# Half-at-a-time state-space tables on GpSimd, and attention scores in two 64-row halves, in a two-layer trunk on one core

## The chip, the core and the metric

One core of one Trainium2 chip. The metric is the device time of one execution in microseconds (us). The engines are named as in the profile: PE is TensorE (PEld its weight loads), DVE is VectorE, ACT is ScalarE, POOL is GpSimd, SP the engine whose queue issues the DMAs. b and h below are numbers of a state-space block and of an attention head.

## The reference

Two layers over a sequence of 256 rows and 2048 columns, all in float32:

```python
proj = x @ w_in[l]                    # 2048 x 4096: q, k, v, u of 1024 columns each
attn = diff_attention(q, k, v, lam)   # 8 heads, each two score maps of 64 columns
ssm  = s5_mixer(u, ...)               # 64 groups of 16 channels, 64 complex states, then a GLU
mix  = concat(group_rms_norm(attn), group_rms_norm(ssm)) @ w_out[l]
x = layer_norm(ALPHA * x + mix)
x = layer_norm(ALPHA * x + square(relu(x @ w_up[l])) @ w_down[l])
```

A head's output is (softmax(q0 k0) - lam softmax(q1 k1)) v, where q0, q1 and k0, k1 are the two 64-column halves of the head, and a row may only see keys of its own 64-row chunk and of earlier ones. The state-space part is a linear recurrence with a complex diagonal factor; the kernel turns it, with tables of cosines and sines of the state's angle, into real scans.

## The kernel before

**Products.** Each float32 product is made of three passes: a weight tile `w` is loaded by DMA (512 KB, 256 rows), ACT rounds it to `wh`, DVE makes the rest `wl = w - wh`, and PE multiplies hi by hi, hi by lo and lo by hi into one accumulator `acc` (`mms`, L209 to 215). There are four `wh` and four `wl` buffers (`WB`), so ACT's rounding waits until PE has used an older one, and PE waits for DVE and ACT. An `acc` instruction has 512 columns.

**A layer.** `mixer` (L836) makes the projections, attention, the state-space part, the GLU and most of `w_out`; `last_chunk` ends it with the layer norm; the MLP follows, 16 chunks of 512 columns, with `acc` matmuls back to back. In the mixer PE's order is written by a small planner (`Flow`): each task yields a test (a time, a free slot, an event), the planner's clock `fl.now` moves on with the instructions put out, and the first ready task of the highest priority goes next. Its constants (`L_PREP`, `L_SCAN`, `L_EXP`, ...) are how long other engines are thought to take. PE runs in exactly this order; the queues of DVE, ACT and POOL are ordered by the compiler's scheduler, and each engine runs its queue in order.

**State space.** 64 groups go in 8 blocks of 8 groups (b = 0 to 7, four pairs of groups each). `ssm_prep` (L455) makes a block's tables on POOL: `abc` (12 instructions of 128x64: the bases times the factor), two memsets, and `tab` (128 x 2 x 4 x 128 numbers) by doubling: step m = 0 to 6 makes n = 1, 2, ... 64 new columns from the n before, six instructions each. ACT spreads `abc` and the bases into `zx` and `cx`; PE transposes `zx` (`zT`) and makes a small kernel `pk`. `ssm_in` (L516) multiplies (PE, `X`, 64 rows at a time), then DVE multiplies X by the tables (16 instructions), scans (8, L542) and multiplies back; `ssm_out` (L552) makes `Y` on PE, DVE adds and the GELU goes through ACT and DVE. Blocks follow each other in one task: X of b+1 comes after Y of b. `tab` has two buffers, `abc` one.

**Attention.** `attn_block` (L583) handles one head and one block of 128 rows: scores `S` into PSUM, one matmul per half with all 128 rows of `kT` against a `qT` whose other half is zero (two `qT` tiles per four heads, written by `to_T`, L818, with `half8`), and one matmul of a one-row mask (`mq`, `mk`) added to it (L598). DVE takes the maximum (`mx`), ACT the exponentials (`pe`), DVE combines the halves; later PE transposes (`pT`) and multiplies by v. Two `S` tiles are in use.

**End of the mixer.** After Y of block 7: GELU, 16 transposes and splits (`uT`, `s`, `gS`), two GLU products, the group norm, and products by `w_out`; whatever of attention and `w_out` is still open fills PE meanwhile.

Of the kernel before, what the change touches and what calls it, by code (L numbers as in the profile page):

```python
# [9 lines left out]
F32 = mybir.dt.float32  # L10
# [8 lines left out]
P = 128  # L19
T = 256  # L20
# [16 lines left out]
UN = 19  # L37
# [13 lines left out]
L_PREP = 7.5  # L51
# [9 lines left out]
class Flow:  # L61
# [53 lines left out]
def trunk(ctx: ExitStack, tc: tile.TileContext, x, w_in, lambda_q1, lambda_k1, lambda_q2, lambda_k2,  # L115
# [13 lines left out]
    ps_a = pool("ps_a", 2, space=PSUM)  # L129
# [35 lines left out]
    half8 = const.tile([P, 2], F32, name="half8")  # L165
    G.memset(half8, 0.0)
    G.memset(half8[0:64, 0:1], HD ** -0.5)
    G.memset(half8[64:128, 1:2], HD ** -0.5)

    mq0 = rawp.tile([1, P], F32, tag="pe", name="mq0", bufs=4)  # L170
    G.memset(mq0, 0.0)
    G.memset(mq0[:, 0:CHUNK], 1.0)
    mk0 = rawp.tile([1, T], F32, tag="pe", name="mk0", bufs=4)
    G.memset(mk0, 0.0)
    G.memset(mk0[:, T - CHUNK:T], -1e30)
    mq = const.tile([1, P], F32R, name="mq")
# [175 lines left out]
    def lay_params(fl, p, l, loaded):  # L352
# [97 lines left out]
        p["nlam"] = nlam  # L450
        ts(p["vec"][:, 0:8], p["vec"][:, 0:8], 1.0 - lam_init, ALU.mult)

    def ssm_prep(fl, p, b):

        qs = slice(4 * b, 4 * b + 4)  # L455

        abc = ssm.tile([P, 4, 4, GC], F32, tag="abc", name="abc")
        tm = [ssm.tile([P, 4, NK // 2], F32, tag="tm", name="tm", bufs=2) for _ in range(2)]
        a_r, a_i = (p["ab"][:, i, qs].unsqueeze(2).to_broadcast([P, 4, GC]) for i in range(2))
        for o, base, s_re, s_im in ((0, p["base"][0], ALU.subtract, ALU.add), (2, p["base"][1], ALU.add, ALU.subtract)):  # L460
            z_r, z_i = base[:, 0, qs], base[:, 1, qs]
# [12 lines left out]
        for g in range(2):  # L474
            act(zx[:, :, :, 0, g], abc[:, 0:2], scale=half[:, g:g + 1])
            act(zx[:, :, :, 1, g], p["base"][0][:, :, qs], scale=half[:, g:g + 1])
            act(cx[:, 0:2, :, g], abc[:, 2:4], scale=half[:, g:g + 1])
            act(cx[:, 2:4, :, g], p["base"][1][:, :, qs], scale=half[:, g:g + 1])
        G.memset(tab[:, 0, :, 0:1], 1.0)
        G.memset(tab[:, 1, :, 0:1], 0.0)  # L480
        for m in range(7):
            n = 1 << m
            er, ei = (p["pw"][:, i, m + 1, qs].unsqueeze(2).to_broadcast([P, 4, n]) for i in range(2))
            u, v = tab[:, 0, :, 0:n], tab[:, 1, :, 0:n]
            t0, t1 = tm[0][:, :, 0:n], tm[1][:, :, 0:n]
# [28 lines left out]
        return bT, k0, cx, tab  # L514

    def ssm_in(fl, p, q, b, u):  # L516

        bT, k0, cx, tab = q
# [33 lines left out]
    def ssm_out(fl, p, q, b, u, h):  # L552

        bT, k0, cx, tab = q
# [28 lines left out]
    def attn_block(fl, p, h, qb, kT, qT, v, i, o, has, need, hold):  # L583

        yield lambda: need[0]() and fl.slot("S")() and fl.slot("hd")() and (qb > 0 or fl.slot("o")())
        if qb == 0:
            hold.append(fl.take("o"))
        give, leave = fl.take("S"), fl.take("hd")
        nk = P * (qb + 1)
        rr = sm.tile([P, 2], F32, tag="rr", name="rr", bufs=3)  # L590
        ri = sm.tile([P, 2], F32, tag="ri", name="ri", bufs=3)
        mx = sm.tile([P, 2], F32, tag="mx", name="mx", bufs=3)
        sp = ps_a.tile([P, 2, T], F32, tag="S", name="S")
        pe = [rawp.tile([P, T], F32, tag="pe", name="pe", bufs=4) for _ in range(2)]
        for s in range(2):
            TE.matmul(out=sp[:, s, 0:nk], lhsT=qT[s][:, h, qb * P:(qb + 1) * P], rhs=kT[:, h, 0:nk],  # L596
                      start=True, stop=False)
            TE.matmul(out=sp[:, s, 0:nk], lhsT=mq, rhs=mk[:, T - nk:T], start=False, stop=True)  # L598
        fl.now += 0.55 * (qb + 1)
        V.reduce_max(out=mx, in_=sp[:, :, 0:nk], axis=AX.X, negate=True)  # L600
        for s in range(2):
            act(pe[s][:, 0:nk], sp[:, s, 0:nk], AF.Exp, bias=mx[:, s:s + 1], accum_out=rr[:, s:s + 1])
        give(L_EXP)

        V.reciprocal(out=ri, in_=rr)
        stt(ri[:, 1:2], ri[:, 1:2], p["nlam"], rr[:, 0:1], ALU.mult, ALU.mult)
        stt(pe[0][:, 0:nk], pe[1][:, 0:nk], ri[:, 1:2], pe[0][:, 0:nk], ALU.mult, ALU.add)
# [3 lines left out]
        for k in range(qb + 1):  # L611
            TE.transpose(ps[:, k], pe[0][:, k * P:(k + 1) * P], ident)
# [205 lines left out]
    def to_T(fl, t, acc, dst, ev):  # L818
# [9 lines left out]
        if len(dst) == 1:  # L828
            act(dst[0][:, :, t * P:(t + 1) * P], ps)
        else:  # L830
            for s in range(2):
                act(dst[s][:, :, t * P:(t + 1) * P], ps, scale=half8[:, s:s + 1])
        give(L_EVAC)
        ev[t].set(L_EVAC)

    def mixer(l, p, xT, first):  # L836
        fl = Flow(tp=2, sx=2, S=2, hd=2, o=2)
# [31 lines left out]
        def attention(i):  # L869
            mA[i] = Split("mA", 1)  # L870
            for h in range(4):
                o = rawp.tile([P, NT, P], F32, tag="o", name="o", bufs=2)
                has, hold = events(NT), []
                for qb in range(NT):
                    need = both(*k_ev[i], *q_ev[i]), both(*v_ev[i])
                    fl.add(3, attn_block(fl, p, h, qb, kT[i], qT[i], v, i, o, has, need, hold))
                fl.add(2, attn_norm(fl, p, 4 * i + h, o, has, lambda hd, m=mA[i]: m(hd % 4), mA_ev[4 * i + h], hold))

        def steps(g, dt=0.65):
# [237 lines left out]
```

## Time and profile before

| | us |
|---|---|
| median of 3 runs | 2340.1 (2339.4 to 2340.41) |
| the profiled execution: its time, its span | 2340.92, 2339.1 |
| PE / DVE / ACT / POOL busy | 2234.1 / 1550.2 / 1080.6 / 446.6 |
| layer 0: first product of X with a table, to Y of block 7 read by DVE | 96.1 to 321.8 |
| from there to the first transpose of the MLP | 321.8 to 484.9 |
| layer 1: the same two stretches | 1246.2 to 1457.9, to 1636.1 |

Busy time is the sum of the instructions' durations without overlaps; a PE instruction's end is modelled, so on PE the distance from one start to the next says more. "Mean ns of one" includes what an instruction waits inside itself. A wait's releaser is who ended it last.

### The profile page before, as it was taken

The page shows a single profiled execution, that of the slowest core. Times are in us where ns is not written, and L with a number is a line of the kernel's source. Part 1 is how long each engine was busy: PE and PEld are TensorE (multiplying, and loading weights), DVE is VectorE, ACT ScalarE, POOL GpSimd, SP SyncE. Part 2 cuts the span into 40 slices and gives each one's busy share as a digit, 9 for nine tenths or more (in the row PEclk, how much of TensorE's full clock was granted, in tenths as well). Part 3 has the DMA queues.
Part 4 walks back from the last instruction along what each step waited for, and adds up shares of the span by engine and source line. Part 5 has one row for each costly group of instructions (what it writes and reads, how often), then busy time and mean ns, then how long its engine had stood idle before and what let it go on. Part 6 is the DMA issues. An engine that isn't in the chain of part 4 may idle for free.

```text
span 2339.1 us, 29790 instructions
## 1 busy us (share of the span) xinstructions
PE 2234.1 (96%) x10836; PEld 1803.0 (77%) x10836; DVE 1550.2 (66%) x2226; ACT 1080.6 (46%) x1521; POOL 446.6 (19%) x990
## 2 busy tenths in 40 slices
PE   8888899999999999999999888999999999999997
PEld 6666677778888878788877667777888888888886
DVE  4667878865555556556677888678555556555557
ACT  4444446354444444444444454654444444444443
POOL 1799900000000001610013983000000000000001
PEclk9998999999999999999999989999999999999998
DMA  8432334666766655565754324465666566666564
GB/s 255 126 97 85 100 123 149 206 183 189 197 199 188 205 179 185 162 195 183 240 157 146 115 73 127 135 195 156 189 189 190 188 196 184 186 194 189 187 198 144
DMA packets 227058, 396.57 MB, mean 170 GB/s; under 512 B 38336, under 2 KB 38496, under 8 KB 226912
## 3 DMA queue, kind: packets, MB, share of 16 engines
q1 hardware_dynamic: 226912, 394.68, 55.1%
q8 instruction: 85, 1.39, 0.2%
q14 instruction: 61, 0.50, 0.1%
HBM read 392.53 MB, written 2.10 MB: 169 GB/s over the span
## 4 chain that ended last, share of the span: by engine, by line
PE 73%; POOL 14%; DVE 6%; issue 3%; DMA 2%; ACT 1%; SPq 1%; DVEq 0%; ACTq 0%; POOLq 0%
PE acc L215 67%; POOL tm L134 9%; POOL tab L134 4%; PE tp L250 2%; PE acc L734 2%; DVE wl L134 1%; DMA w<-in_w_in 1%; DVE res L150 1%; DVE wk L134 1%; POOL abc L134 1%; ACT wh L153 1%; PE S L596 1%; DMA w<-in_w_up 1%; DVE wk L542 1%; PE S L598 0%
## 5 line engine op out<-in xcount | busy, mean ns | idle before, releaser
L134 DVE TENSOR_TENSOR wl<-w,wh 128x1024 fp32r<-128x1024 f32 x714 | 881.3, 1236 | 626.4 <-ACT wh L153 611.6
L153 ACT ACTIVATE wh<-w 128x1024 fp32r<-128x1024 f32 x714 | 755.7, 1060 | 829.7 <-PE acc L215 780.9
L215 PE MATMUL acc<-wh,xTh 128*128 128x512 f32 x1440 | 571.9, 404 | 9.7 <-ACT wh L153 6.3
L215 PE MATMUL acc<-wl,xTh 128*128 128x512 f32 x1440 | 571.0, 397 | 2.8 <-DVE wl L134 2.6
L215 PE MATMUL acc<-wh,xTl 128*128 128x512 f32 x1440 | 569.5, 396 | 0.0
L215 PE MATMUL acc<-wh,hidh 128*128 128x512 f32 x1024 | 405.6, 396 | 2.7 <-DVE res L134 1.9
L215 PE MATMUL acc<-wh,hidl 128*128 128x512 f32 x1024 | 400.0, 391 | 0.0
L215 PE MATMUL acc<-wl,hidh 128*128 128x512 f32 x1024 | 399.2, 390 | 0.0
L215 PEld LDWEIGHTS acc<-wh,xTh 128*128 128x128 f32 x1440 | 276.2, 192 | 74.0 <-ACT wh L153 7.9
L215 PEld LDWEIGHTS acc<-wl,xTh 128*128 128x128 f32 x1440 | 276.5, 192 | 60.1 <-DVE wl L134 6.5
L215 PEld LDWEIGHTS acc<-wh,xTl 128*128 128x128 f32 x1440 | 276.0, 192 | 58.1
L215 PEld LDWEIGHTS acc<-wh,hidh 128*128 128x128 f32 x1024 | 192.5, 188 | 41.5 <-DVE res L134 2.4
L215 PEld LDWEIGHTS acc<-wh,hidl 128*128 128x128 f32 x1024 | 192.2, 188 | 40.9
L215 PEld LDWEIGHTS acc<-wl,hidh 128*128 128x128 f32 x1024 | 192.6, 188 | 38.2
L134 DVE TENSOR_TENSOR res<-res,acc 128x512 f32<-128x512 f32 x288 | 196.8, 683 | 17.3 <-PE acc L215 15.5
L298 POOL TENSOR_TENSOR rs<-rs,mhalf 128x1 f32<-128x1 f32 x8 | 7.8, 974 | 1019.9 <-DVE rs L147 1019.9
L134 POOL TENSOR_TENSOR tm<-tab,pw 128x4 f32<-128x4 f32 (+6 forms) x448 | 191.1, 447 | 16.4
L134 POOL TENSOR_TENSOR tab<-tm 128x4 f32<-128x4 f32 (+6 forms) x224 | 108.4, 484 | 16.8
L445 POOL TENSOR_TENSOR lel<-ebase,lsl 128x2 f32<-128x2 f32 x2 | 1.4, 712 | 447.2 <-DVE lsl L443 447.2
L134 DVE TENSOR_TENSOR wk<-X,tab 128x128 f32<-128x128 f32 x256 | 54.8, 282 | 32.7 <-POOL tab L134 20.8
L153 ACT ACTIVATE raw<-acc 128x512 f32<-128x512 f32 x80 | 47.0, 587 | 61.5 <-PE acc L215 61.4
L134 POOL TENSOR_TENSOR tm<-base,ab 128x64 f32<-128x64 f32 x128 | 55.9, 456 | 29.1 <-DVE base L134 24.6
(186 smaller groups left out, 2101.7 us busy)
## 6 DMA issues: line engine op xcount, KB each, us to landing
w<-in_w_up SPq DMA_DIRECT2D x256, 512.0 KB, 3.9
w<-in_w_down SPq DMA_DIRECT2D x256, 512.0 KB, 4.9
w<-in_w_in SPq DMA_DIRECT2D x128, 512.0 KB, 4.0
w<-in_w_out SPq DMA_DIRECT2D x64, 512.0 KB, 4.2
w<-in_glu_w SPq DMA_DIRECT2D x16, 512.0 KB, 4.1
gb<-in_ln_g SPq DMA_DIRECT2D x8, 512.0 KB, 8.8
gb<-in_ln_b SPq DMA_DIRECT2D x8, 512.0 KB, 10.0
out<-res SPq DMA_DIRECT2D x8, 256.0 KB, 2.1
```

The costliest lines, as they stand in the source:

```text
L134: (eng or V).tensor_tensor(out=out, in0=in0, in1=in1, op=op)
L150: V.scalar_tensor_tensor(out=out, in0=a, scalar=s, in1=b, op0=op0, op1=op1)
L153: S.activation(out=out, in_=in_, func=func, **kw)
L215: TE.matmul(out=acc, lhsT=a[:, c], rhs=b, start=(first and i == 0), stop=(last and i == 2))
L250: TE.transpose(ps[:, i], src(i), ident)
L298: G.tensor_tensor(out=self.rs, in0=self.rs, in1=mhalf[:, 0:1], op=ALU.pow)
L445: G.tensor_tensor(out=el, in0=ebase[:, 0:2], in1=sl, op=ALU.pow)
L542: V.tensor_tensor_scan(out=g[:, r], data0=ml, data1=s[:, r], initial=0.0, op0=ALU.mult, op1=ALU.add)
L596: TE.matmul(out=sp[:, s, 0:nk], lhsT=qT[s][:, h, qb * P:(qb + 1) * P], rhs=kT[:, h, 0:nk], start=True, stop=False)
L734: TE.matmul(out=acc[t], lhsT=(lo if i == LH else hi)[:, c], rhs=(wl if i == HL else wh)[:, k % 2], start=seen[t] == 0, stop=seen[t] == 3 * ...
```

## The change

- **Tables.** `half_prep` makes `abc` for four blocks at once (12 instructions of 128x256) and `fine`, the first 16 table columns of these four blocks (steps m = 0 to 3, 24 instructions of 16 to 128 columns). Per block `ssm_prep` copies its part of `fine` into `tab` by ACT and makes steps m = 4 to 6 on POOL (18 instructions). The first half is made in `lay_params`, which for layer 1 runs during the MLP of layer 0; the second half in front of block 4.
- **POOL's time in PE's order.** The planner keeps `fl.pool`, the time at which POOL is done (`L_HALF`, `L_TAB`); `ssm_in` of a block is put out only when it has come.
- **Scores.** `attn_head` makes both row blocks of a head in one PSUM tile of two banks (one such tile, where there were two of one bank): eight score matmuls become four, each with 64 rows of `qT` and `kT` (rows 0 to 63 for the first half, 64 to 127 for the second). The mask matmuls go; one DVE memset per head writes -1e30 into the masked quarter (64 rows, 256 columns). `qT` is one tile with the scale in `to_T`. The planner knows one score slot per head and three head slots.
- `UN` 19 to 18 tiles; constants of the planner; `half8`, `mq`, `mk` go.

```diff
-UN = 19
+UN = 18
...
-L_PREP = 7.5
+L_PREP = 3.0
+L_HALF = 26.0
+L_TAB = 14.0
...
-    ps_a = pool("ps_a", 2, space=PSUM)
+    ps_a = pool("ps_a", 1, space=PSUM)
...
+        p["halves"] = 1
+        half_prep(fl, p, 0)
...
+    def turn_on(tm, o_r, o_i, u, v, er, ei, less=ALU.subtract, more=ALU.add):
+
+        mul(tm[0], u, er, G)
+        mul(tm[1], v, ei, G)
+        tt_(o_r, tm[0], tm[1], less, G)
+        mul(tm[0], v, er, G)
+        mul(tm[1], u, ei, G)
+        tt_(o_i, tm[0], tm[1], more, G)
...
+    def half_prep(fl, p, i):
+
+        qs = slice(16 * i, 16 * i + 16)
+        abc = ssm.tile([P, 4, 16, GC], F32, tag="abc", name="abc")
...
+            turn_on(tm, abc[:, o], abc[:, o + 1], base[:, 0, qs], base[:, 1, qs], a_r, a_i, *signs)
+        fine = ssm.tile([P, 2, 16, 16], F32, tag="fine", name="fine")
+        G.memset(fine[:, 0, :, 0:1], 1.0)
+        G.memset(fine[:, 1, :, 0:1], 0.0)
+        for m in range(4):
...
+        p["half"] = abc, fine
+        fl.pool = max(fl.now, fl.pool) + L_HALF
+
     def ssm_prep(fl, p, b):
 
+        if b % 4 == 0 and p["halves"] <= b // 4:
+            half_prep(fl, p, b // 4)
+            p["halves"] = b // 4 + 1
...
+        hs = slice(4 * (b % 4), 4 * (b % 4) + 4)
+        abc, fine = p["half"]
+        prepared = fl.after(max(0.0, fl.pool - fl.now) + L_PREP)
...
-            act(zx[:, :, :, 0, g], abc[:, 0:2], scale=half[:, g:g + 1])
+            act(zx[:, :, :, 0, g], abc[:, 0:2, hs], scale=half[:, g:g + 1])
...
-        G.memset(tab[:, 0, :, 0:1], 1.0)
-        G.memset(tab[:, 1, :, 0:1], 0.0)
-        for m in range(7):
+        act(tab[:, :, :, 0:16], fine[:, :, hs])
+        tm = tm_tiles(4, NK // 2)
+        for m in range(4, 7):
...
+        fl.pool = max(fl.now, fl.pool) + L_TAB
+        ready = fl.pool
+        yield prepared
+        yield fl.slot("sx")
...
-        bT, k0, cx, tab = q
+        bT, k0, cx, tab, ready = q
+        yield lambda: fl.now >= ready
...
+        yield lambda: need[0]() and fl.slot("S")() and fl.slot("hd", NT)() and fl.slot("o")()
...
+        sp = ps_a.tile([P, 2, 2 * T], F32, tag="S", name="S")
+        at = [0, P]
+        for qb in range(NT):
+            nk = P * (qb + 1)
+            for s in range(2):
+                rows = slice(64 * s, 64 * s + 64)
+                TE.matmul(out=sp[:, s, at[qb]:at[qb] + nk], lhsT=qT[rows, h, qb * P:(qb + 1) * P],
+                          rhs=kT[rows, h, 0:nk], start=True, stop=True, skip_group_check=True)
+        fl.now += 1.0
+
+        V.memset(sp.rearrange("p s (b k) -> p s b k", k=T)[0:CHUNK, :, :, CHUNK:2 * CHUNK], -1e30)
+        for qb in range(NT):
...
+            V.reduce_max(out=mx, in_=blk, axis=AX.X, negate=True)
+            for s in range(2):
+                act(pe[s][:, 0:nk], blk[:, s], AF.Exp, bias=mx[:, s:s + 1], accum_out=rr[:, s:s + 1])
...
+        give(2 * L_EXP)
...
-        fl = Flow(tp=2, sx=2, S=2, hd=2, o=2)
+        fl = Flow(tp=2, sx=2, S=1, hd=3, o=2)
```

**How the instructions move.** The first place is POOL's queue at block 0 of layer 0. Before the change: the end of `abc` and the first doublings, from one column on (`tm` holds the partial products, `pw` the powers of the angle).

```order
L134 TENSOR_TENSOR tm<-base,ab 128x4x16 x2
L134 TENSOR_TENSOR abc<-tm 128x64
L134 TENSOR_TENSOR tm<-tab,pw 128x4 x2
L134 TENSOR_TENSOR tab<-tm 128x4
L134 TENSOR_TENSOR tm<-tab,pw 128x4 x2
L134 TENSOR_TENSOR tab<-tm 128x4
L134 TENSOR_TENSOR tm<-tab,pw 128x4x2 x2
L134 TENSOR_TENSOR tab<-tm 128x4x2
```

With the change: the last row of the half that is made ahead (`fine`, its first 16 columns), and the start of what is left to block 0 itself:

```order
L136 TENSOR_TENSOR fine<-tm 128x16x8
L136 TENSOR_TENSOR tm<-tab,pw 128x4x16 x2
L136 TENSOR_TENSOR tab<-tm 128x4x16
L136 TENSOR_TENSOR tm<-tab,pw 128x4x16 x2
L136 TENSOR_TENSOR tab<-tm 128x4x16
L136 TENSOR_TENSOR tm<-tab,pw 128x4x32 x2
L136 TENSOR_TENSOR tab<-tm 128x4x32
```

`abc` and the four smallest doublings have left the block for the half; the steps from 16 columns on have stayed, and every block has them. The second place is PE's queue at the first head of layer 0 before the change, behind the first X of block 2 (`mk`, `mq` are the mask's two rows):

```order
L215 MATMUL acc<-wh,xTl 128x512
L528 MATMUL X<-uT,bT 128x128 x4
L596 MATMUL S<-kT,qT 128x128
L598 MATMUL S<-mk,mq 128x128
L596 MATMUL S<-kT,qT 128x128
L598 MATMUL S<-mk,mq 128x128
L596 MATMUL S<-kT,qT 128x256
L598 MATMUL S<-mk,mq 128x256
```

and with the change:

```order
L202 MATMUL acc<-wh,xTl 128x512
L508 MATMUL zT<-ident,zx 128x128 x4
L518 MATMUL pk<-cx,zx 32x32 x8
L607 MATMUL S<-kT,qT 128x128 x2
L607 MATMUL S<-kT,qT 128x256 x2
L202 MATMUL acc<-wh,xTh 128x512
```

The eight score and mask matmuls of a head have become four in a row. The third place is DVE's queue at a head in layer 0 with the change; the memset stands between the scores and their maximum:

```order
L136 TENSOR_TENSOR o<-o,ss 128x256
L611 MEMSET S 64x4x64
L619 TENSOR_REDUCE mx<-S 128x2
L623 RECIPROCAL ri<-rr 128x2
L619 TENSOR_REDUCE mx<-S 128x2
L152 SCALAR_TENSOR_TENSOR ri<-ri,nlam,rr 128x1
L152 SCALAR_TENSOR_TENSOR ge<-uT,vecT,Y 128x128 x2
```

Before, the first row of a head on DVE was its maximum.

## Rows read from the trace of the kernel before

**Rows 1.** The page: busy time by engine (part 1), and the whole chain by engine (part 4).
```profile
PE 2234.1 (96%) x10836; PEld 1803.0 (77%) x10836; DVE 1550.2 (66%) x2226; ACT 1080.6 (46%) x1521; POOL 446.6 (19%) x990
PE 73%; POOL 14%; DVE 6%; issue 3%; DMA 2%; ACT 1%; SPq 1%; DVEq 0%; ACTq 0%; POOLq 0%
```

**Rows 2.** Busy time by stretch: from:to, length, each engine (instructions), clock, DMA, GB/s.
```profile
96.10:321.80 225.70, 191.77 (x1218) 145.16 (x1219) 181.12 (x390) 99.72 (x208) 178.44 (x411) 0.90 0.33 100
1246.20:1457.90 211.70, 189.63 (x1222) 142.88 (x1223) 181.76 (x389) 94.80 (x200) 144.09 (x338) 0.93 0.36 108
1457.90:1636.10 178.20, 172.55 (x797) 137.18 (x798) 136.00 (x217) 92.26 (x163) 5.59 (x10) 0.99 0.51 161
```

**Rows 3.** The chain of waits from 96 to 322 us, its shares by line.
```profile
by line: POOL tm L134 43.8%; POOL tab L134 18.6%; PE acc L215 9.0%; issue 8.5%; POOL abc L134 5.6%; DVE wk L134 3.6%; DVE wk L542 2.3%; DVE wl L134 1.7%; PE Y L569 1.5%; PE X L528 1.1%; POOL ss L635 0.9%; ACT wh L153 0.8%; POOL ss L147 0.5%
```

**Rows 4.** Waits from 96 to 322 us: who <- whom: us in total, times, longest.
```profile
DVE wk L134 <- POOL tab L134: 20.8, 6, 9.2
ACT zx L153 <- POOL abc L134: 48.4, 7, 11.6
ACT pe L153 <- DVE mx L600: 11.3, 4, 4.7
```

**Rows 5.** Timeline of POOL, layer 0: first and last table instruction (start us, us, ...).
```profile
73.56 0.80 POOL L134 TENSOR_TENSOR tm<-base,ab 128x64 f32<-128x64 f32 x1 [7.39 <-DVE base L134]
...
291.68 1.07 POOL L134 TENSOR_TENSOR tab<-tm 128x256 f32<-128x256 f32 x1
```

**Rows 6.** POOL by form, whole run: ... xcount | busy us, mean ns | idle before.
```profile
L134 POOL TENSOR_TENSOR tm<-tab,pw 128x256 f32<-128x256 f32 x64 | 52.6, 841 | 2.3
L134 POOL TENSOR_TENSOR tm<-tab,pw 128x128 f32<-128x128 f32 x64 | 32.6, 530 | 2.3
L134 POOL TENSOR_TENSOR tm<-tab,pw 128x64 f32<-128x64 f32 x64 | 31.4, 510 | 2.5
L134 POOL TENSOR_TENSOR tm<-tab,pw 128x16 f32<-128x16 f32 x64 | 18.4, 307 | 2.3
```

**Rows 7.** Timeline of PE: the projected inputs of a block, then one head's scores.
```profile
1269.64 0.39 PE L215 MATMUL acc<-wl,xTh 128*128 128x512 f32 x1
1269.86 0.39 PE L215 MATMUL acc<-wh,xTl 128*128 128x512 f32 x1
1270.18 0.71 PE L528 MATMUL X<-uT,bT 64*128 64x128 f32 x8
1270.83 0.50 PE L215 MATMUL acc<-wh,xTh 128*128 128x512 f32 x1
...
1511.37 0.39 PE L596 MATMUL S<-kT,qT 128*128 128x128 f32 x2
...
1512.61 0.50 PE L215 MATMUL acc<-wh,gSh 128*128 128x512 f32 x1
...
1513.41 0.59 PE L596 MATMUL S<-kT,qT 128*128 128x256 f32 x2
...
1515.18 0.50 PE L215 MATMUL acc<-wh,gSh 128*128 128x512 f32 x1
```

**Rows 8.** DVE by form from 96 to 322 us.
```profile
L134 DVE TENSOR_TENSOR wl<-w,wh 128x1024 fp32r<-128x1024 f32 x44 | 56.9, 1294 | 5.9 <-ACT wh L153 5.6
L542 DVE TENSOR_TENSOR_SCAN wk<-magL,wk 128x128 f32<-128x128 f32 x64 | 29.6, 528 | 0.0
L600 DVE TENSOR_REDUCE mx<-S 128x2 f32<-128x512 f32 x4 | 2.7, 680 | 1.2 <-PE S L598 1.2
L511 DVE COPY k<-pk 32x64 f32<-32x64 f32 x14 | 3.0, 212 | 0.1
```

**Rows 9.** DVE by form from 297 to 322 us, after POOL's last table.
```profile
L542 DVE TENSOR_TENSOR_SCAN wk<-magL,wk 128x128 f32<-128x128 f32 x8 | 2.6, 407 | 0.0
```

**Rows 10.** The page, part 5: the residual add.
```profile
L134 DVE TENSOR_TENSOR res<-res,acc 128x512 f32<-128x512 f32 x288 | 196.8, 683 | 17.3 <-PE acc L215 15.5
```

**Rows 11.** Timeline of ACT in the MLP of layer 0, where layer 1's tables start.
```profile
980.30 0.69 ACT L153 ACTIVATE cx<-abc,half 128x128 f32<-128x128 f32 x2 [6.36 <-POOL abc L134]
```

More of the change, by code (lines that the diff above doesn't have):

```diff
@@ L450, in lay_params, with tm_tiles @@
         p["nlam"] = nlam
+        p["halves"] = 1
+        half_prep(fl, p, 0)
         ts(p["vec"][:, 0:8], p["vec"][:, 0:8], 1.0 - lam_init, ALU.mult)
+    def turn_on(tm, o_r, o_i, u, v, er, ei, less=ALU.subtract, more=ALU.add):
[5 more added lines that the diff above has]
+        tt_(o_i, tm[0], tm[1], more, G)
+    def tm_tiles(*shape):
+        return [ssm.tile([P, *shape], F32, tag="tm", name="tm", bufs=2) for _ in range(2)]
@@ L552, in ssm_out @@
     def ssm_out(fl, p, q, b, u, h):
-        bT, k0, cx, tab = q
+        bT, k0, cx, tab, _ = q
         yield fl.slot("sx")
@@ L581, in ssm_out @@
         stt(u.rearrange("p h k -> p (h k)"), y2, 1.0, y, ALU.add, ALU.mult)
[L583 to L607, printed above, removed]
@@ new lines, in attn_head @@
+    def attn_head(fl, p, h, kT, qT, v, i, o, has, need, hold):
+        yield lambda: need[0]() and fl.slot("S")() and fl.slot("hd", NT)() and fl.slot("o")()
+        hold.append(fl.take("o"))
+        give, leave = fl.take("S"), [fl.take("hd") for _ in range(NT)]
+        sp = ps_a.tile([P, 2, 2 * T], F32, tag="S", name="S")
[9 more added lines that the diff above has]
+        for qb in range(NT):
+            nk = P * (qb + 1)
+            rr = sm.tile([P, 2], F32, tag="rr", name="rr", bufs=5)
+            ri = sm.tile([P, 2], F32, tag="ri", name="ri", bufs=5)
+            mx = sm.tile([P, 2], F32, tag="mx", name="mx", bufs=5)
+            pe = [rawp.tile([P, T], F32, tag="pe", name="pe", bufs=6) for _ in range(2)]
+            blk = sp[:, :, at[qb]:at[qb] + nk]
+            V.reduce_max(out=mx, in_=blk, axis=AX.X, negate=True)
+            for s in range(2):
+                act(pe[s][:, 0:nk], blk[:, s], AF.Exp, bias=mx[:, s:s + 1], accum_out=rr[:, s:s + 1])
+            V.reciprocal(out=ri, in_=rr)
+            stt(ri[:, 1:2], ri[:, 1:2], p["nlam"], rr[:, 0:1], ALU.mult, ALU.mult)
+            stt(pe[0][:, 0:nk], pe[1][:, 0:nk], ri[:, 1:2], pe[0][:, 0:nk], ALU.mult, ALU.add)
+            fl.add(3, attn_block(fl, h, qb, pe[0], ri, v, i, o, has, need, leave[qb]))
+        give(2 * L_EXP)
@@ L608, in attn_block @@
+    def attn_block(fl, h, qb, pe, ri, v, i, o, has, need, leave):
         yield fl.slot("tp", dt=L_P)
@@ L827, in to_T @@
         fl.now += 0.44
[L828 to L832, printed above, removed]
+        act(dst[:, :, t * P:(t + 1) * P], ps, scale=scale)
         give(L_EVAC)
@@ L873, in attention, with steps @@
                 has, hold = events(NT), []
-                for qb in range(NT):
-                    need = both(*k_ev[i], *q_ev[i]), both(*v_ev[i])
-                    fl.add(3, attn_block(fl, p, h, qb, kT[i], qT[i], v, i, o, has, need, hold))
+                need = both(*k_ev[i], *q_ev[i]), both(*v_ev[i])
+                fl.add(3, attn_head(fl, p, h, kT[i], qT[i], v, i, o, has, need, hold))
                 fl.add(2, attn_norm(fl, p, 4 * i + h, o, has, lambda hd, m=mA[i]: m(hd % 4), mA_ev[4 * i + h], hold))
-        def steps(g, dt=0.65):
+        def steps(g, dt=0.68):
             while True:
```

61 lines of the change are left out of this document (18 added, 43 removed).

## The prediction, blind

> **What bounds the kernel now.** I read the page first. PE is busy 96% of the span, but POOL, busy only 19%, holds 14% of the chain that ended last [rows 1]: its work must lie in few places where everything waits for it. The stretch table finds them. From the first product of X with a table to the last Y, in both layers, POOL is busy 178.4 of 225.7 us and 144.1 of 211.7 us, the granted clock falls to 0.90 and 0.93, and PE is busy 85% and 90% of the time; in the stretch behind, shown for layer 1, POOL does next to nothing, PE is at 97% and the clock at 0.99 [rows 2]. In the first stretch POOL's lines are 68% of the chain (tm, tab, abc) [rows 3]. POOL works there without a break: its first table instruction starts at 73.6 us, its last ends at 292.8 us, 219 us for eight blocks, 27.4 us each [rows 5]. What waits: DVE for `tab`, and ACT, whose queue stands at `zx` for 48.4 us in seven waits, with the `wh` roundings that feed PE behind it [rows 4].
>
> The reader should see one more thing: DVE is the next bound, and close. It is busy 181.1 and 181.8 us of these stretches, 80% and 86% [rows 2]. So POOL's work can shrink by more than the time will.
>
> **The change, part by part.**
>
> *Tables.* Half of the blocks costs 12 instructions of 256 columns at 0.84 us for `abc` (10.1 us), then six each of 16, 32, 64 and 128 columns for `fine`: 0.31, about 0.34 (an estimate between its neighbours), 0.51 and 0.53 us, 10.1 us together; 20.2 us per half. A block keeps six each of 64, 128 and 256 columns: 6 x (0.51 + 0.53 + 0.84) = 11.3 us [rows 6]. A layer needs 2 x 20.2 + 8 x 11.3 = 131 us where 219 us went by. In a block's 27 us POOL now works 11.3, and the order leaves room for the second half between X of blocks 3 and 4. I take POOL off the path except at the start of layer 0. There block 0 needs a whole half and its own steps, 31.5 us from 73.6 us on, so its tables stand at 105 us, where DVE's first product came at 96.1: **+9 us**. In layer 1 the first half lies in the MLP; no change there.
>
> *The stretch of layer 0 is then DVE's.* By the order, between the same two instructions DVE now has 4 more `wl` (1.29 us each, 5.2 us), 8 residual adds (0.68, 5.5 us), 6 more maxima (0.68 at most, 3.3 us for both sizes), 7 memsets, and some 24 small steps of heads and norms (about 6 us) [rows 8, 10]. A memset of 256 columns in PSUM is not in the trace; the nearest rows are a copy of 64 columns out of PSUM, 0.21 us, and a maximum over 512, 0.68 us [rows 8]. It is nearer the copy, since nothing is reduced: 0.3 us, 2.1 us for seven; by the ends 1.5 to 4.8. That is 22 us more. Against it: while POOL works, a scan takes 0.53 us, after POOL's last table 0.41 [rows 8, 9]. 64 scans lose some 8 us to POOL's company, `wl` and the adds a few more; with POOL's work in the stretch down from 178 us to about 100 I take 5 us off. DVE's work: 181 + 22 - 5 = 198 us. How full can its queue be? The ends are 0.86, as in layer 1 where POOL still spoils it [rows 2], and 1.00. Since most of the present holes go back to POOL, I take 0.92: 215 us, from 105 to 320 us. The stretch gives **-10.7 us** in length.
>
> *Layer 1's stretch.* DVE gets 8 more `wl`, 5 residual adds and 2 more maxima, 17 us; 181.8 + 17 - 5 = 194 us, at 0.92 211 us where 211.7 stand [rows 2]: **0**.
>
> *What has moved is gone from behind.* The longer order of the stretch swallows work that stood after it. From Y of block 7 to the MLP PE has 487 `acc` matmuls where it had 574 in layer 0, 523 for 616 in layer 1; back to back an `acc` takes 0.22 to 0.23 us from start to start [rows 7], so 20 and 21 us leave. Of scores, half a head and three heads stand there now, four and four before.
>
> *A head's scores on PE.* Before: 1.24 us for the first row block (1511.37 to 1512.61) and 1.77 us for the second, 3.0 us [rows 7]. After: X is the same kind of work, four matmuls of 64 rows and 128 columns, two at a time in the two halves of the array, and it takes 0.65 us, 0.33 a pair; 0.32 us instead of 0.22 to 0.23 pass before its start [rows 7]. A pair of 128 and one of 256 columns then take 0.33 + 0.65 + 0.09, at most 1.1 us: 1.9 us less per head, 31 us for 16 heads on PE. Where DVE sets the pace this saving is covered and I count it at nothing; behind it I count it: 12.0 - 0.6 = 11 us in layer 0 and 12.0 - 3.3 = 9 us in layer 1. If the halves ran one after the other, a head would take about 2 us, 1 us more.
>
> The Trainium skill ("TensorEngine Tiling (Array Packing)", "Key Properties") says that a change of tiling mode drains TensorE, which speaks against 16 more such visits. The 0.09 us ahead of X is what this trace shows of it; by the rule and that row it is 1.4 us in all, without the rule nothing.
>
> *What is lost behind.* The GLU's inputs need 16 transposes, each evacuated by ACT, and the old order laid attention and `w_out` matmuls between; the new order has them in one row, right after a Y. I put 8 us of idle PE in layer 0 and 5 us in layer 1 (estimate: the GELU of one block and eight evacuations of 0.6 to 0.7 us). Tails: layer 0 -20 - 11 - 1 (transposes moved ahead) + 8 = **-24 us**; layer 1 -21 - 9 + 5 = **-25 us**.
>
> *The MLP of layer 0.* There ACT's queue stood 6.4 us at block 1's `cx` for POOL's `abc`, with `wh` roundings behind it [rows 11]; what PE lost by it lies between nothing and those 6.4 us, nearer the latter, since the `wh` buffers run dry meanwhile. The half makes `abc` of blocks 0 to 3 at once, so this wait should go; ACT's new copy of `fine` comes some 20 us after POOL's start and may wait a little: **-5 us**. ACT also loses two `qT` writes per 128 rows and gains 16 copies; both are covered.
>
> **Sum.** +9 - 10.7 + 0 - 24 - 25 - 5 = -56 us against the profiled execution's 2340.9, which is 0.8 us above the median of 2340.1. I predict **2284 us** (-2.4%).
>
> **Rivals.**
>
> *DVE runs full.* With its queue at 1.00 the stretches take 198 and 194 us, 17 and 17 less: 2250. For it: DVE would have a backlog throughout. Against: in-order queues that wait for each other, as ACT's `pe` for `mx` [rows 4].
>
> *DVE stays as patchy as it is.* At 0.80 and 0.86 [rows 2] the stretches take 247 and 226 us, 32 and 15 more: 2331. For it: layer 1 is at 0.86 although POOL has made two blocks ahead. Against: the longest holes are POOL's.
>
> *The score saving does not show.* Without it the tails give 20 us less: 2304. That is so if the halves run one after the other, against [rows 7], or if the readers of the scores set the pace. The Trainium skill (same page, "PSUM Bottleneck") says that tiling speeds up TensorE but not the emptying of PSUM; maximum and exponentials per head are indeed as before, plus a memset. It would make the time this 2304.
>
> *Slower: one score tile.* A head's scores now wait until ACT has read the last exponential of the head before, which waits for DVE's maximum in DVE's full queue; on PE all that is behind waits too. Today ACT waits for `mx` up to 4.7 us at a time, 11.3 us in all, with two tiles [rows 4]. If every head cost PE such 4.7 us, 16 x 4.7 = 75 us: 2359. It decides from 56 / 16 = 3.5 us a head on. Against: in the new order of layer 0 all but the last two heads have some 15 us or more of other PE work between them, counted by `acc` matmuls.
>
> **How the numbers follow.** The forecast, 2264 to 2304 without the third rival's reason, 0.45; DVE full 0.18; DVE patchy 0.18; no score saving 0.11; one score tile 0.08. To hold 8 in 10 the range goes from 2240, below the first rival by the memset's and the lock-free scans' bounds, to 2330, the second rival's time; left out are the slower case and the outer halves of the two DVE cases. A measurement of this kernel tells 0.2% (4.7 us) from no change. Faster than that: the first four cases but the tail of the patchy one, 0.87; the same 0.05; slower 0.08.
>
> **What would show it.** Right: POOL's share of the chain under 4%; `zx` waits for `abc` only at the halves; DVE over 88% busy from X to the last Y; a head's scores about 1 us on PE; clock nearer 1.0. Wrong: DVE holes that end at POOL, gaps on PE ahead of `S`, ACT standing at `tab<-fine`, or a stretch of DVE over 230 us.

## The result, and the profile after

The change runs in 2315.3 us (median of 4 runs, 2313.33 to 2316.09) where the kernel before took 2339.75 us beside it (4 runs, 2338.37 to 2340.41): ratio 0.9895, 95% interval 0.9878 to 0.9912, a gain of 24.5 us. Forecast were 2284 us and a gain of 56. The direction was right and the time lies in the range, but less than half of the gain came. The profiled execution took 2316.09 us, its span 2314.4.

The page of the change, parts 1 and 4, beside [rows 1]:

```profile
PE 2203.0 (95%) x10772; PEld 1781.9 (77%) x10772; DVE 1542.6 (67%) x2242; ACT 1076.9 (47%) x1527; POOL 330.4 (14%) x527
PE 77%; DVE 12%; POOL 3%; issue 3%; ACT 2%; DMA 1%; SPq 1%; DVEq 0%; ACTq 0%; POOLq 0%
```

POOL has left the chain (14% to 3%, under 4% as forecast), and DVE's share has doubled. The busy times by stretch, beside [rows 2] (from:to, length, PE, PEld, DVE, ACT, POOL, granted clock, DMA share, GB/s), with the pieces from block 3's first product to block 4's under the stretch that holds them:

```profile
108.60:339.90 231.30, 198.84 (x1288) 150.62 (x1289) 193.29 (x437) 110.55 (x250) 109.96 (x187) 0.90 0.36 110
192.60:246.00 53.40, 50.30 (x287) 39.37 (x285) 40.30 (x84) 29.95 (x74) 21.28 (x33) 0.92 0.41 121
339.90:476.10 136.20, 130.49 (x598) 104.46 (x599) 108.61 (x170) 66.98 (x103) 3.75 (x6) 0.97 0.50 159
476.10:1234.80 758.70, 751.74 (x3403) 618.51 (x3402) 458.12 (x512) 349.02 (x397) 60.76 (x79) 1.00 0.62 191
1234.80:1457.20 222.40, 198.28 (x1315) 152.36 (x1315) 193.17 (x415) 107.23 (x224) 95.09 (x160) 0.96 0.40 122
1305.90:1359.30 53.40, 47.44 (x270) 37.46 (x269) 41.55 (x81) 28.17 (x69) 28.92 (x51) 0.94 0.39 118
1457.20:1611.30 154.10, 142.79 (x670) 114.35 (x671) 120.85 (x200) 78.21 (x141) 7.08 (x10) 0.97 0.51 158
```

The stretches did not get shorter: 231.3 us where 225.7 stood, and 222.4 for 211.7. The gain lies behind them. DVE has 193 us of work in each, much as forecast, but fills only 84% and 87% of them, not 92%. One piece stands out in both layers: from block 3 to block 4 pass 53.4 us, where the other blocks take 19 to 30, and in it DVE works 40.3 and 41.6 us while PE works 50.3 and 47.4.

That piece was written into the order. Three rows of the change's timelines, the start of the second half on POOL, its last table instruction of block 4, and PE's X of block 4:

```profile
164.09 1.20 POOL L136 TENSOR_TENSOR tm<-base,ab 128x256 f32<-128x256 f32 x2
...
197.93 1.59 POOL L136 TENSOR_TENSOR tab<-tm 128x256 f32<-128x256 f32 x1
...
245.27 0.71 PE L540 MATMUL X<-uT,bT 64*128 64x128 f32 x8
```

The tables are ready at 199.5 us; X comes 46 us later. The planner starts to count the half's 26 us and the block's 14 only when X of block 3 has been put out, and holds X of block 4 until they are over. In the run POOL had begun that half at 164 us, before X of block 3 (188 to 193 us).

The waits of PE and of DVE in layer 0's stretch of the change (who <- whom: total, times, longest):

```profile
PE Y L581 <- DVE wk L136: 13.3, 8, 5.3
PE pT L635 <- DVE pe L152: 8.3, 4, 5.2
...
DVE wk L136 <- PE X L540: 10.8, 7, 3.4
DVE o L136 <- POOL ss L658: 10.1, 4, 4.3
```

The same waits before the change, from 96 to 322 us, with PE's at X, which is gone with the change:

```profile
PE X L528 <- DVE wk L134: 17.0, 7, 9.2
PE Y L569 <- DVE wk L134: 13.4, 7, 4.1
PE pT L612 <- DVE pe L150: 4.8, 2, 4.7
DVE wk L134 <- PE X L528: 3.1, 2, 1.9
DVE o L134 <- POOL ss L635: 2.1, 2, 1.2
```

No wait for `tab` is left of the 20.8 us in [rows 4] but one of 1.3 us, and PE's 17.0 us at X are gone. But PE waits at Y as long as before, PE and DVE wait for each other more at `pT` and at X, and DVE's product `o` by `ss` waits for POOL's power, which stands behind table steps. So PE stands idle in the two stretches as long as before: 32.5 and 24.1 us, where it was 33.9 and 22.1. PE waits nowhere at S for the one score tile.

Prices, by the change's timeline of PE in layer 1 ([rows 7] show the same before) and by DVE's forms in layer 0's stretch:

```profile
1478.63 0.40 PE L202 MATMUL acc<-wh,gSl 128*128 128x512 f32 x1
1478.96 0.93 PE L607 MATMUL S<-kT,qT 64*128 64x128 f32 x8
1479.81 0.51 PE L202 MATMUL acc<-wh,gSh 128*128 128x512 f32 x1
...
L554 DVE TENSOR_TENSOR_SCAN wk<-magL,wk 128x128 f32<-128x128 f32 x64 | 26.0, 470 | 0.0
L619 DVE TENSOR_REDUCE mx<-S 128x2 f32<-128x512 f32 x7 | 4.7, 667 | 0.0
...
L611 DVE MEMSET S<- 64x256 f32 x7 | 1.9, 272 | 1.3 <-PE S L607 1.1
```

A head's scores take 0.85 us (1478.96 to 1479.81) where 3.0 stood [rows 7]; the memset takes 0.27 us (0.3 taken); a scan 0.47 us, between the 0.53 of [rows 8] and the 0.41 of [rows 9].

### The profile page after: what moved, and what is told of

Same layout as the page of the kernel before. It is cut to its first block, busy times and chain, and to the rows that moved or that the text cites. A ratio compares the mean times of both kernels' runs of the same rounds, so it can differ in the third digit from the quotient of the medians.

```text
span 2314.4 us, 29243 instructions
## 1 busy us (share of the span) xinstructions
PE 2203.0 (95%) x10772; PEld 1781.9 (77%) x10772; DVE 1542.6 (67%) x2242; ACT 1076.9 (47%) x1527; POOL 330.4 (14%) x527
## 4 chain that ended last, share of the span: by engine, by line
PE 77%; DVE 12%; POOL 3%; issue 3%; ACT 2%; DMA 1%; SPq 1%; DVEq 0%; ACTq 0%; POOLq 0%
PE acc L202 71%; DVE wk L136 3%; DVE wl L136 3%; POOL tm L136 2%; PE tp L237 2%; PE acc L757 2%; DVE wk L554 2%; DVE res L152 1%; ACT wh L155 1%; PE Y L581 1%; DMA w<-in_w_in 1%; PE X L540 1%; DVE res L136 0%; PE pT L642 0%; DVE st L712 0%
## 5 line engine op out<-in xcount | busy, mean ns | idle before, releaser
L136 POOL TENSOR_TENSOR tm<-tab,pw 128x64 f32<-128x64 f32 (+2 forms) x192 | 123.6, 664 | 177.1 <-ACT tab L155 171.0
L136 DVE TENSOR_TENSOR wk<-X,tab 128x128 f32<-128x128 f32 x256 | 54.4, 278 | 17.6 <-PE X L540 16.3
L136 POOL TENSOR_TENSOR tab<-tm 128x64 f32<-128x64 f32 (+2 forms) x96 | 61.5, 641 | 6.7
L202 PE MATMUL acc<-wh,mAh 128*128 128x512 f32 x128 | 52.9, 414 | 1.8 <-DVE res L152 1.8
```

The costliest lines, as they stand in the source:

```text
L136: (eng or V).tensor_tensor(out=out, in0=in0, in1=in1, op=op)
L202: TE.matmul(out=acc, lhsT=a[:, c], rhs=b, start=(first and i == 0), stop=(last and i == 2))
```

## The experiments

Beside each, the kernel before was timed again; its median lay between 2337.7 and 2338.7 us, so small differences go by the ratios. "The hole" is the room for POOL's second half between X of blocks 3 and 4. T1 says that the hole took the gain; T2, that PE is full in the hole, and that elsewhere PE and DVE wait for each other wherever the order reckons DVE too fast; T3, that cheaper scores let the order run ahead of a POOL that is no faster.

### The scores alone

The kernel before with the change's `attn_head`, one `qT`, one score tile, and the 0.68 us (0.65 before) that the planner reckons for a step of products; tables, `L_PREP` and `UN` as before.

> The kernel before with the change's scores alone (halves of 64 rows, one score tile, mask by VectorE, one qT, the 0.68 us step); tables and their place in the order as before. If the parts simply add, as my sum took it: the stretches stay POOL's, 226 and 212 us or a few us more, a head's scores take 0.9 us on PE instead of 3.0 and only the heads behind the stretch count, so about 20 us less than before, 2320, and the tables then give only about 5 us. Rival (the tables carry the change, the scores are covered by waits for POOL): 2330 to 2340. Rival (the single score tile costs something by itself): over 2340.

2351.27 us, ratio 1.006 (1.0047 to 1.0072): slower. Its stretches, and ACT's longest wait in layer 0's:

```profile
96.70:330.40 233.70, 185.30 (x1192) 141.42 (x1192) 174.53 (x392) 95.57 (x202) 174.76 (x411) 0.87 0.32 93
...
1259.60:1470.20 210.60, 177.42 (x1200) 136.26 (x1201) 184.62 (x394) 93.55 (x198) 149.20 (x338) 0.91 0.37 107
...
ACT zx L153 <- POOL abc L134: 59.7, 6, 14.6
```

PE's work in the run falls from 2234.1 to 2206.3 us, and its idle time grows by more: in the two stretches from 56 us (225.7 - 191.8 and 211.7 - 189.6) to 82. ACT stands at `zx` 59.7 us where 48.4 stood [rows 4]. To see whether the halves cost this or the order, the next run gives the tables more time in the order:

```diff
-L_PREP = 7.5
+L_PREP = 12.0
```

> The run with the scores alone (2351), and the order reckons 12 us instead of 7.5 us for a block's tables, so that each block gets about 72 acc matmuls where it had about 65. T3, the scores alone are slower because their shorter price lets the order run further ahead of GpSimd, whose 27 us a block are still there, so that ACT stands at zx for abc (59.7 us in layer 0) with GELU and roundings behind it: with time given back, the zx waits fall and the total is 2325 to 2338, at or below the kernel before. Rival (the halves, the one tile or the mask cost by themselves, wherever they stand): 2345 to 2355.

2334.85 us, ratio 0.9991 (0.9982 to 1.0). The same wait:

```profile
ACT zx L153 <- POOL abc L134: 34.3, 4, 11.5
```

The time is back at that of the kernel before and the wait has fallen, as T3 expected: with less PE time per head the planner's clock had run ahead of POOL's tables. The halves themselves show no cost that can be measured.

The like for the kernel before, with its own scores (`L_SCAN`, the time reckoned from X to Y, from 12.5 to 14.0):

> The kernel before with 14.0 instead of 12.5 us reckoned from X to Y and nothing else. If GpSimd's 27.4 us a block set its stretches, giving each block more matmuls fills PE's idle time there (34 us in layer 0, 22 us in layer 1) as well, and it gains 5 to 15 us without any of the change: 2325 to 2335. If the later Y only pays once the tables are off the path: 2338 to 2345.

2335.18 us, ratio 0.9986 (0.9977 to 0.9995), a gain of 3 us, at the edge of the first expectation. So, each with more time in its order, though by different constants, old scores give 0.9986 and new scores 0.9991: without the new tables the new scores show no gain that can be measured.

### What the scores are worth in the change

```diff
-            for s in range(2):
+            for _ in range(3):
+                for s in range(2):
...
```

> The change with each head's four score matmuls issued three times (the same products, written over), the order else the same: a head then takes about 2.6 us on PE instead of 0.85, near the 3.0 us of before, +28 us of PE over 16 heads. It prices the saving that the halves bring. By my sum (covered in the stretches by VectorE, counted behind them: 3.5 heads there): 6 to 10 us more, 2321 to 2326. If PE sets the pace everywhere: 28 us more, 2343. If all is covered: 2315.

2317.8 us, ratio 0.9915 (0.9901 to 0.9928). A head's scores, in layer 1's tail:

```profile
1493.33 0.40 PE L202 MATMUL acc<-wh,gSl 128*128 128x512 f32 x1
1493.66 2.24 PE L608 MATMUL S<-kT,qT 64*128 64x128 f32 x24
1495.83 0.50 PE L202 MATMUL acc<-wh,gSh 128*128 128x512 f32 x1
```

That is 2.17 us a head, not 2.6: 1.32 us more, 21 us for 16 heads. The time rose by 2.5 us, and the intervals of this run and of the change overlap. The stretches and tails of this run:

```profile
107.90:337.90 230.00, 199.34 (x1400) 153.37 (x1400) 197.43 (x437) 109.94 (x250) 109.40 (x185) 0.95 0.37 110
337.90:476.00 138.10, 132.74 (x613) 106.55 (x614) 108.58 (x170) 66.89 (x103) 3.75 (x6) 0.96 0.49 157
...
1234.50:1455.50 221.00, 203.54 (x1395) 158.02 (x1396) 193.07 (x416) 106.98 (x224) 97.41 (x160) 0.97 0.41 123
1455.50:1612.00 156.50, 146.65 (x715) 118.18 (x715) 121.50 (x198) 76.84 (x140) 7.25 (x10) 0.96 0.49 154
```

The tails grew by 1.9 and 2.4 us, near the 5.3 us that the four heads in them cost at 1.32; the stretches, with twelve heads, did not grow. The 21 us went two ways: PE's idle time in the run fell by 10 us (111.4 to 101.4), and its busy time rose by 12 us (2203.0 to 2215.1) instead of 21, so that other matmuls took less time. In layer 0's stretch seven heads, 9 us, raised the busy time by 0.5 us, and the granted clock there is 0.95 where the change had 0.90. So the 2.5 us are what the work cost with that clock; what it would cost at an equal clock is not shown.

The tables with scores at 2.2 us are thus worth some 20 us. A kernel with the new tables and the scores of before, at 3.0 us a head, was not run; the last 0.8 us of a head have no price.

### The hole, and the time to Y

```diff
-        fl.pool = max(fl.now, fl.pool) + L_HALF
+        fl.pool = max(fl.now, fl.pool) + (L_HALF if i == 0 else 0.0)
```

> The change, but the order reckons nothing for GpSimd's second half, so X of block 4 is put out about 85 acc matmuls sooner (570 instead of 657 in layer 0, 4806 instead of 4890 in layer 1). T1, the hole between blocks 3 and 4 is what kept VectorE at 0.84 and 0.87: the pitch of these two blocks goes from 53.4 to about 30 us in both layers, VectorE's 13 and 12 us of idle time there go, and the total falls by some 20 us to 2295. T2, the hole cost only VectorE, and TensorE was full in it (50.3 of 53.4 us): the pitch shortens, but the matmuls taken out of the hole come back behind the stretch; TensorE's idle time, 32 us in layer 0's stretch and 24 us in layer 1's, stays, and the total is 2310 to 2320.

2310.08 us, ratio 0.9882 (0.9868 to 0.9895). Layer 0's stretch, the piece from block 3 to 4, what follows up to layer 1's first product, and layer 1's stretch:

```profile
107.10:314.20 207.10, 177.84 (x1204) 133.41 (x1203) 179.91 (x404) 98.36 (x212) 103.20 (x182) 0.93 0.37 108
190.10:218.00 27.90, 24.59 (x162) 17.98 (x162) 27.18 (x64) 14.93 (x38) 14.48 (x25) 0.89 0.40 114
314.20:1230.80 916.60, 898.33 (x4082) 735.50 (x4083) 580.55 (x714) 427.47 (x537) 66.37 (x89) 0.99 0.61 185
1230.80:1432.30 201.50, 177.98 (x1200) 136.60 (x1200) 176.91 (x393) 95.89 (x204) 97.09 (x160) 0.93 0.38 111
```

The piece shrinks from 53.4 to 27.9 us and the stretch by 24 us, yet layer 1's first product comes only 4 us sooner (1230.8 for 1234.8): the matmuls that filled the hole now stand behind Y of block 7. PE's idle time in the stretches is 52.8 us where the change had 56.6. T2's number came, T1's did not. The gain over the change is 5 us between the medians and 3 us by the ratios, whose intervals overlap: filling the hole alone shows no clear gain.

Now with each block given more matmuls as well:

```diff
-L_SCAN = 12.5
+L_SCAN = 14.0
```

> As the run without the hole, and the order reckons 14.0 us instead of 12.5 us from X of a block to its Y, so that each block gets about 70 acc matmuls of its own instead of about 60 (Y of block 7 of layer 0 at acc 861, nearly as in the change at 864, blocks evenly apart). T2, TensorE waits at Y and at the transposes for a VectorE that has more work per block than the order gives it time: PE's waits at Y (13.3 us in layer 0, 7.3 in layer 1) fall to a few us, TensorE's idle time in the two stretches falls from 56 to about 30 us, the total is about 2290. T1, only the hole counted: the same time as the run without the hole, within 5 us.

2298.09 us, ratio 0.9829 (0.9814 to 0.9844): 17 us below the change (15 by the ratios), a gain of 41 us where the change had 24.5. Stretches, and PE's waits in the whole run:

```profile
107.10:321.50 214.40, 189.60 (x1265) 144.16 (x1265) 189.34 (x422) 106.17 (x232) 113.06 (x184) 0.94 0.38 114
...
1222.40:1430.40 208.00, 188.14 (x1263) 145.47 (x1265) 181.09 (x398) 102.42 (x212) 93.75 (x160) 0.95 0.40 120
...
PE pT L635 <- DVE pe L152: 18.0, 11, 5.0
...
PE Y L581 <- DVE wk L136: 3.1, 2, 2.3
```

PE's waits at Y fell to 3.1 us (20.6 in the whole run of the change), its idle time in the stretches to 44.7; the 30 expected were not reached. DVE fills 0.88 and 0.87 of the stretches, not more than without the hole alone (0.87 and 0.88).

The missing corner, the later Y with the hole left in:

> The change with 14.0 instead of 12.5 us reckoned from X to Y and nothing else: the hole between blocks 3 and 4 stays. It is the corner that is missing beside the change (2315), the run without the hole (2310) and the run with both (2298). If the later Y is what counts (T2): PE's waits at Y fall as in the run with both, total 2298 to 2306. If both are needed (with the hole, later Y push block 7 of layer 0 past the last filler, acc 864, so that PE runs dry behind): 2310 to 2325.

2312.47 us, ratio 0.9896 (0.9882 to 0.9909), as the change: both are needed. With the hole, Y of block 7 of layer 0 comes when no other product is left: PE has no `acc` matmul at all between X (336.1 us) and Y (346.2 us) of block 7, and waits:

```profile
335.20:350.60 15.40, 9.71 (x68) 6.37 (x68) 14.26 (x46) 5.37 (x20) 1.05 (x2) 0.61 0.00 0
```

### More of PE, less of DVE

The even version with the scores three times:

> The run with evenly spaced blocks (2298) with each head's score matmuls issued three times, the order else the same: about 28 us more of PE work, as in the run with the change (there +2.5). If the even version is bound by TensorE and the halves' saving is now worth its price: 2315 to 2326. If TensorE still waits for VectorE there and the extra matmuls fall into its 45 us of idle time in the stretches: 2300 to 2306.

2296.09 us, ratio 0.9825 (0.9812 to 0.9838), below both expectations: 16 heads with PE work added cost nothing that can be measured in the even version. Then DVE's work. The last product and sum of a block's state go, so that the kernel leaves out a part of the state:

```diff
-        mul(m4, m4, cos)
-        add(m2, m2, m4)
```

> The run with evenly spaced blocks (2298) without the last product and the last sum on VectorE of every block's state (the part of its second half that goes with the cosine is left out): 0.69 + 0.78 us less on VectorE, 16 times, 23.5 us; the order else the same. If VectorE sets the pace of the even stretches: about 20 us less, 2275 to 2280. If VectorE and TensorE wait for each other at single places, which an equal share of work does not move: 5 to 14 us less, 2284 to 2293. If VectorE is covered: 2296 to 2300.

2282.47 us, ratio 0.976 (0.9746 to 0.9774): 15.6 us less for 23.5 us of DVE work, between the first two expectations. In the change itself:

> The change (2315) with the same product and sum left out of every block (the part of the state's second half that goes with the cosine): 0.68 + 0.73 us, 16 times, 22.7 us less on VectorE. By my prediction's step (the stretches are as long as VectorE's work over a fixed fill): 22.7 / 0.92, about 25 us less, 2290. By T2 (the hole is TensorE's, 53 us a layer whatever VectorE does, and VectorE paces only the seven other blocks): 10 to 18 us less, 2297 to 2305. If VectorE is covered: 2313 to 2317.

2289.66 us, ratio 0.9794 (0.9779 to 0.981): 25.6 us less. The stretches and the pieces from block 3 to 4:

```profile
105.90:324.70 218.80, 189.14 (x1288) 144.59 (x1289) 186.85 (x420) 109.87 (x250) 112.06 (x187) 0.94 0.39 117
184.70:234.90 50.20, 48.22 (x286) 37.50 (x286) 38.26 (x81) 30.01 (x75) 23.18 (x36) 0.97 0.43 129
...
1218.30:1430.50 212.20, 196.46 (x1315) 151.53 (x1315) 181.94 (x399) 106.91 (x224) 96.52 (x160) 0.96 0.42 127
1287.90:1340.10 52.20, 47.35 (x274) 36.67 (x274) 39.04 (x78) 27.71 (x69) 28.49 (x49) 0.97 0.40 121
```

And PE's waits at Y in the whole run, first in the change, then here:

```profile
PE Y L581 <- DVE wk L136: 20.6, 14, 5.3
...
PE Y L579 <- DVE wk L136: 6.1, 2, 5.5
```

The total is my prediction's number (25), and T2's 10 to 18 missed. But the holes behaved as T2 said: 53.4 to 50.2 and 52.2 us. The stretches lose 12.5 and 10.2 us, 22.7 together, as much as the instructions taken from DVE had cost, and 18.3 of it outside the holes. That fits a DVE that sets the pace outside the holes, though in the change it is filled there to only 0.86 (153.0 of 177.9 us, layer 0) and 0.90 (151.6 of 169.0). It does not show it, for two reasons. The two instructions end the chain from X to Y, and PE's waits at Y fell from 20.6 to 6.1 us: a shorter chain would do the same, and no run took as much DVE work from another place. And in layer 0's stretch the same 1288 matmuls took 189.1 us instead of 198.8, 9.7 of the 12.5 us, with a granted clock of 0.94 instead of 0.90; PE's idle time there fell by only 2.8 us.

### Four that did not help

The norm's product 5 us later, away from POOL's power:

```diff
+        yield fl.after(5.0)
         mul(o, o, ss.unsqueeze(2).to_broadcast([P, NT, P]))
-        yield fl.slot("tp", dt=L_NORM)
+        yield fl.slot("tp", dt=3.0)
```

> The change, with VectorE's multiplication o by ss put into the order 5 us later (its transposes 8 us after the power instead of 6), so that it does not stand at VectorE's head while GpSimd's power waits behind table steps: 10.1 us in layer 0 and 4.4 us in layer 1 in the change. If these waits were on the path that sets the end: 5 to 14 us less, 2301 to 2310. If they only shift (VectorE's idle time is made up in TensorE's filled time): 2312 to 2318.

2311.24 us, ratio 0.9886 (0.9872 to 0.9899): the interval overlaps the change's; not settled. On the even version:

> The run with evenly spaced blocks (2298) and the norm's product 5 us later (alone: 2311 for 2315). If the two gains add: 2294. If evenly spaced blocks already take those waits (10.1 us for GpSimd's power in layer 0 fell to 3.7 us there): 2296 to 2300.

2301.91 us, ratio 0.9852 (0.9838 to 0.9865): no gain there. With 12.5 for 9.6 us to the transposes of the probabilities as well (`L_P`):

> The run with evenly spaced blocks (2298), with the norm's product put 5 us later as in the run of that name, and 12.5 us instead of 9.6 us reckoned from a row block's scores to the transposes of its probabilities. PE waits 22 us at these transposes for VectorE's pe and ri in the even run. T2 (PE idles wherever the order reckons VectorE too fast): these waits go below 10 us, total 2284 to 2292. Rival (the later transposes hold the next head's scores and run into the tail): 2295 to 2305.

2298.77 us, ratio 0.9829 (0.9816 to 0.9843): no gain, although PE's waits for `pe` at these transposes fell from 18.0 to 12.8 us, and although DVE fills 0.90 and 0.91 of the stretches (0.88 and 0.87 in the even version):

```profile
107.30:322.50 215.20, 189.13 (x1268) 143.28 (x1269) 194.26 (x421) 105.27 (x229) 110.88 (x184) 0.95 0.39 116
...
1229.80:1430.30 200.50, 188.19 (x1260) 145.51 (x1260) 182.06 (x398) 102.56 (x212) 97.29 (x160) 0.95 0.41 124
```

Layer 1's stretch is 7.5 us shorter and begins 7.4 us later. And layer 1 with 16 us from X to Y on the even version:

> The run with evenly spaced blocks (2298), with 16 us instead of 14 us reckoned from X to Y in layer 1 alone, where more filler is left (82 acc matmuls a block to its end, where layer 0 has 70): blocks about 78 apart. T2: TensorE's 20 us of idle time in layer 1's stretch shrink further, 2290 to 2296. If layer 1 is now limited elsewhere (the tail behind it grows as much): 2297 to 2303.

2301.46 us, ratio 0.9849 (0.9836 to 0.9863): layer 1's stretch grew from 208.0 to 226.8 us and what followed shrank by only 14 us.

## Why the prediction was right and wrong

| term | forecast | measured |
|---|---|---|
| first product of layer 0 | 105 | 108.6 |
| stretch of layer 0 | 215 | 231.3 |
| tail of layer 0 | 139 | 136.2 |
| end of the tail to layer 1's first product | -5 | -2.6 (758.7, before 761.3) |
| stretch of layer 1 | 211 | 222.4 |
| tail of layer 1 | 153 | 154.1 |

**Right.** GpSimd was the bound and leaves the path; DVE is next. Its work in the stretches (198 and 194 us forecast, 193.3 and 193.2 measured), the tails, the memset and a head's scores on PE came within a few us or a tenth of one. The single score tile, the rival on the slower side, shows no wait of PE at S.

**The signs** set beforehand were mixed. POOL's share of the chain (3%), the waits of `zx` for `abc` (none in layer 0's stretch, one of 3.9 us in layer 1's) and a head's scores on PE (0.85 us) came as for "right". DVE's 84% and 87% (over 88% was asked), the clock of layer 0's stretch (0.90 as before; layer 1's rose from 0.93 to 0.96), a stretch of 231.3 us and ACT once 10.8 us at `tab<-fine` came as for "wrong".

**The step that failed** is the fill of DVE's queue: "Since most of the present holes go back to POOL, I take 0.92". It was 0.84 and 0.87, which makes 16.3 and 11.4 us of the 32 that the sum missed. The present holes did go back to POOL (DVE's waits for `tab` in layer 0 fell from 20.8 to 1.3 us), but others came in their place: the order's own hole, and more waits of PE and DVE for each other. About half of that shortfall lies in one place per layer: at 0.92 the pieces from block 3 to 4 would have taken 43.8 and 45.2 us (40.3 and 41.6 over 0.92) instead of 53.4 each, 18 us; the blocks outside them would have taken 16 us less (153.0 and 151.6 over 0.92 against 177.9 and 169.0); some 6 us of these 34 come back, since DVE has less work than forecast. The first part could be read ahead: the prediction itself says that the order leaves room for the second half between X of blocks 3 and 4, and prices that room at nothing. In it PE works 50 and 47 of 53 us, so it is PE's length rather than DVE's, as the run with less DVE work shows (50.2 and 52.2 us).

What I had not thought of is the second side: filling the hole alone gives 3 to 5 us, not clear of the noise, since its matmuls then stand behind the stretch. Only with the blocks evenly spaced as well, each with more PE work of its own, come 15 to 17 us. What is left of the miss, some 14 us from the even version to the forecast, stays open. A fuller DVE is no simple source: the run with later transposes has it at 0.90 and 0.91, and PE's waits for `pe` at 12.8 us for 18.0, in the time of the even version. So a fuller DVE by itself does not make this kernel faster, as the step had it. In the change itself two smaller terms missed too: the first product came 3.6 us later than reckoned, and from the tail to layer 1 only 2.6 of 5 us came, while in the MLP ACT now waits 4.8 us for `fine`, which the prediction put at a little; that this wait is the cause is not shown.

**Right number, for mixed reasons.** The tails fell by 26.9 and 24.1 us as forecast (24, 25), of which I put 20 down to scores. Most of these 20 us are heads that moved into the stretches: four heads at 3.0 us stood behind each, and the trace has one and three left (the prediction took half a head and three). For those behind, the price counts: with the score matmuls three times the tails grew by 4.3 us. In the stretches it does not, as the prediction took it. The rival "the score saving does not show" put the tails 20 us longer, and they were not; what the runs bear out of it is that the work saved on most heads brought little, 2.5 us for the 21 us put back, and that at a higher clock. The Trainium skill ("TensorEngine Tiling (Array Packing)", "PSUM Bottleneck") says that tiling speeds up TensorE and not the emptying of PSUM; the trace agrees, with a head's scores at 0.85 us for 3.0 and a maximum over 512 columns of PSUM at 0.67 us for 0.68 [rows 8].

**The mode change.** From the last `acc` to S pass 0.33 us, where 0.23 lie between two `acc`: 0.1 us, 1.6 us for 16 heads, near the 1.4 forecast. The same page ("Key Properties") says that a change of mode drains the engine; the row agrees that some time passes, and it is small.

**The chance.** Faster was given 0.87 and came; the time is in the upper half of the range, 11 us from the rival "the score saving does not show" (2304) and 16 us from "DVE stays as patchy as it is" (2331). By its reason it is nearer the second, whose fills of 0.80 and 0.86 lie just under those measured; the time lies in the range by the width that this rival gave it, not by the step that set its middle.

## What to carry to other kernels

When an engine leaves the path of a kernel whose order is written ahead, the order's own constants can become the bound: look in the new order for the place where a reckoned wait leaves a hole, and price it by the engine that works in it. A fill of the next engine is not a number to choose; two engines that wait for each other leave both idle, and here only the hole filled and the work spaced evenly, together, brought 15 to 17 us back. And a saving on a covered engine is worth little: 21 us of PE work put back on the scores cost 2.5 us, and alone the cheaper scores made the kernel 0.6% slower, because a cheaper step let the order run ahead of the engine that was late. The even version, 0.9829 of the time before, is the one to keep.

## What the runs showed that I had not expected

More PE work can cost nothing, and not only by filling idle time. The two stretches of the even version with the scores three times:

```profile
108.60:322.70 214.10, 195.58 (x1361) 150.59 (x1361) 190.24 (x422) 105.88 (x232) 112.76 (x183) 0.95 0.38 114
...
1221.70:1426.50 204.80, 187.73 (x1327) 146.81 (x1329) 181.89 (x399) 101.79 (x212) 93.24 (x160) 0.97 0.41 122
```

Some 21 us of matmuls were added (16 times 1.32), but PE's busy time rose only from 2197.2 to 2206.6 us and its idle time fell by about 10; the granted clock is 0.95 and 0.97 in the stretches where it was 0.94 and 0.95, and 0.986 over the run for 0.981. The other matmuls took less time. The same shows in the change with the scores three times, and in the change with less DVE work, where the same matmuls of layer 0's stretch took 9.7 us less. That the clock is the cause is an inference from these rows, not shown by a run of its own; it means that a gain or a price in this document can hold a part that is the clock's.
